# A depthwise convolution's three terms moved to ScalarE, its sums made in two long operations, and one Strassen-like step taken a unit later

## The chip, the cores and the metric

One Trainium2 chip, one core of it. The metric is the device time of the whole program in microseconds. In rows of the profile, PE is TensorE (matmuls), PEld its weight loads, DVE is VectorE, ACT is ScalarE, POOL is GpSimd and SP is SyncE, which here only issues DMAs. A "q" behind a name means the engine's sequencer. L896 is line 896 of the kernel file.

## The reference

A two-layer encoder on 256 tokens with 2048 features, all in float32. Each layer is an attention mixer and then a gated feed-forward block, each with a residual sum. The change touches the feed-forward block alone:

```python
D_FF = 5632
def conv_ffn(x, w_up, conv_w, conv_b, w_down):
    h = jnp.einsum("bsd,df->bsf", x, w_up)
    g, u = h[..., :D_FF], h[..., D_FF:]
    gp = jnp.pad(g, ((0, 0), (1, 1), (0, 0)))
    g = conv_w[0] * gp[:, :-2] + conv_w[1] * gp[:, 1:-1] + conv_w[2] * gp[:, 2:] + conv_b
    return jnp.einsum("bsf,fd->bsd", jax.nn.gelu(g) * u, w_down)
```

The gate `g` is convolved along the tokens with three taps for each feature, goes through the GELU and is multiplied with `u`.

## The kernel before

Every float32 matmul is made of three: operands are split into a high part (a rounded copy, made by a cast on ACT) and a low part (the rest, made by a subtraction on VectorE), and the products high x high, high x low and low x high are added in PSUM. Weights come from memory as units of 128 x 1024 (`raw`, five buffers, loaded on SP's queue); `split` makes `wh` on ACT (L231) and `wl` on VectorE (L234), four buffers each. A unit feeds 12 matmuls of 512 columns (`a_unit`, L195 to L197).

The up projection runs in 11 groups for each layer (`up_group`), each for 512 gate features (x = 0) and 512 `u` features (x = 1). A group takes eight steps over the contraction. The first four steps do both sides (`u` = 0 to 3), then come four for the gate side alone and four for the other side. At step `UPK` a group does not multiply plainly: `column_forms` combines the weights of the two sides with four sums on VectorE (L951, L952, L954, L955), splits the combinations as three pairs `wh`/`wl` and one quarter (`form`, from the tile `t`), and `seven_products` makes seven block products instead of eight (L977 to L979), 21 matmuls instead of 24. Four extra PSUM banks take products that are added to both sides later (`extra_parts`, `scaled_parts`).

When the gate side is done, VectorE evicts it (L878, into a tile of the tag `sc`), transposes it in blocks of 32 (L279), and 16 DMAs move the blocks (L273, twelve on POOL, four on SP) into `sides[0]`, a tile `qk` of four feature blocks by 256 tokens. The `u` side follows the same way through a tile `z` into `sides[1]`. Work that is to come later is put off with `later` and issued by `tick`: the convolution (`convolved`) is issued two ticks after the gate's eviction and so falls into the start of the next group, and `multiplied` comes there too. In three groups of each half (`HALVES`, groups 1 to 3 of the half) `multiplied` also makes the sums L324 to L327 and splits them for the down projection.

The convolution works on each of four feature blocks: ACT makes the middle term with the bias (L896), VectorE adds the two outer terms with a fused multiply-add each (L897, L899), over 255 tokens. Then one ACT operation makes the GELU of all four (L901).

The order of instructions on each engine is set by a scheduler at build time; it follows priorities and its own estimate of times. Each engine runs its list in order, so a waiting instruction holds up all behind it.

Of the kernel before, what the change touches and what calls it, by code (L numbers as in the profile page):

```python
# [29 lines left out]
AF = mybir.ActivationFunctionType  # L30
ALU = mybir.AluOpType
# [3 lines left out]
SEQ = 256  # L35
# [12 lines left out]
RAW = 5  # L48
AHEAD = 4
LAST = 2  # L50
UPK = 2
HALVES = ((0, 6, (1, 2, 3)), (6, 11, (1, 2, 3)))


# [17 lines left out]
def trunk_kernel(ctx: ExitStack, tc, a, out):  # L72
    nc = tc.nc
    V, S, G, T = nc.vector, nc.scalar, nc.gpsimd, nc.tensor
# [11 lines left out]
    def nm(s):  # L86
        uid[0] += 1
        return f"{s}_{uid[0]}"
# [22 lines left out]
    def load(name, shape, src=None, pool=const, tag=None, eng=G):  # L111
        t = pool.tile(list(shape), F32, name=name, **({"tag": tag} if tag else {}))
        tc.keep_in_program_order(eng.dma_start(t, a[name] if src is None else src))
        return t

    def tps(tag, bufs):
        return psum.tile([P, 512], F32, name=nm(tag), tag=tag, bufs=bufs)
# [164 lines left out]
    def y_tile(src, gain, kt, pin=False):  # L282
        y = acts.tile([P, 2, SEQ], F32R, name=nm("yT"), tag="yT", bufs=KT)
        dst = [y[:, x, :] for x in range(2)]
        if len(src.shape) == 3:
            dst = [d.rearrange("p (t q) -> p t q", t=2) for d in dst]
        split_scaled(*dst, src, gain[:, kt:kt + 1], pin)
        return y
# [16 lines left out]
    def turned_rows(c, gain, res):  # L305
# [6 lines left out]
        def tiles():  # L312
            for j in range(4):
                res[c * 4 + j] = y_tile(pf.rearrange("p (t j) q -> p j t q", t=2)[:, j], gain, c * 4 + j)
            if res is formed.get("of") and c == UPK // 2:
                y_forms(pf.rearrange("p (t j) q -> p j t q", t=2), gain)
# [4 lines left out]
    def form_sums(a11, a21, a12, a22):  # L321

        f = tmp.tile([P, 4, P], F32, name=nm("sums"), tag="scc")
        V.tensor_tensor(f[:, 0], a21, a22, op=ALU.add)  # L324
        V.tensor_tensor(f[:, 1], f[:, 0], a11, op=ALU.subtract)
        V.tensor_tensor(f[:, 2], a11, a21, op=ALU.subtract)
        V.tensor_tensor(f[:, 3], a12, f[:, 1], op=ALU.subtract)  # L327
        return f

    def y_forms(src, gain):  # L330

        y = tmp.tile([P, 2, 2, P], F32, name=nm("yf"), tag="ry")
        for k in range(2):
            S.activation(y[:, k], src[:, UPK % 2 * 2 + k], AF.Copy, scale=gain[:, 2 * UPK + k:2 * UPK + k + 1])
        f = form_sums(*(y[:, k, t] for k in range(2) for t in range(2)))
        form = []
        for x, tag in enumerate(("R", "Rq")):
            high = tmp.tile([P, 2, P], F32R, name=nm("form"), tag="t0")
            low = const.tile([P, 2, P], F32R, name=nm("form"), tag=tag, bufs=1)
            split(high, low, f[:, 2 * x:2 * x + 2])  # L340
            form += [(high[:, k], low[:, k]) for k in range(2)]
        formed["form"] = form

    def row_factor(pin=False, late=False):

        ss = tmp.tile([P, 2], F32, name=nm("ss"), tag="ss")
        ins = V.tensor_reduce(ss, ssq_now[0], axis=AX.X, op=ALU.add)
        if pin:
            tc.keep_in_program_order(ins)
        return rsqrt_mean(ss, D, "rstd", const, late=late)  # L350
# [63 lines left out]
    def quad(slot, dtype=F32):  # L414
        return att.tile([P, 4, SEQ], dtype, name=nm("qk"), tag=f"qk{slot}", bufs=1)
# [40 lines left out]
    def qk_tiles(srcs, act, rs, orders, slot):  # L456

        return [qk_sum(ps, r, order, slot + x)
                for x, (ps, r, order) in enumerate(zip(gemm_b(srcs, act), rs, orders))]
# [182 lines left out]
    def new_sc():  # L642
        return att.tile([P, 2, 512], F32, name=nm("sc"), tag="sc", bufs=1)
# [100 lines left out]
    convw = load("convw", (P, 2, 3, FT))  # L744
    convb = load("convb", (P, 2, FT))
# [89 lines left out]
    def up_group(layer, j, yT, rstd, prod, *more):  # L835
# [23 lines left out]
        for u in range(4):  # L859
            if not j and u == 2:  # L860
                rstd.append(row_factor())
            if u == UPK:
                extra += [tps("s", 2), tps("tp", 2), tps("tp", 2), tps("s", 2)]
# [6 lines left out]
        for x in range(2):  # L870
            for u in range(4, 8):
                a_unit(pss[x], src[x], u, yT, KT)
                if u % 2 == 1:
                    tick()
            z = (tmp.tile([P, 8, P], F32, name=nm("z"), tag="z", bufs=1) if x else
                 new_sc().rearrange("p t (f k) -> p (t f) k", k=P))
            for t in range(2):
                out = V.scalar_tensor_tensor(z.rearrange("p (f t) k -> p t f k", t=2)[:, t],  # L878
                                       pss[x][t].rearrange("p (f k) -> p f k", k=P), rstd[0][:, t:t + 1],
                                       sums[x][t].rearrange("p (f k) -> p f k", k=P), op0=ALU.mult, op1=ALU.add)  # L880
                if t:
                    tc.keep_in_program_order(out)
            sides[x] = quad(2 * x)
            turned(z.rearrange("p b k -> p (b k)"), sides[x].rearrange("p f (t k) -> p (f t) k", k=P), (3,))
            if not x:
                later(2, lambda: convolved(layer, j, sides))
        later(2, lambda: multiplied(j, sides, prod, *more))

    def convolved(layer, j, sides):

        g4, c4 = sides[0], quad(4)
        sides[2] = c4
        for i in range(4):
            f = 4 * j + i
            g, c = g4[:, i, :], c4[:, i, :]
            S.activation(c, g, AF.Identity, scale=convw[:, layer, 1, f:f + 1], bias=convb[:, layer, f:f + 1])  # L896
            V.scalar_tensor_tensor(c[:, 1:SEQ], g[:, 0:SEQ - 1], convw[:, layer, 0, f:f + 1],  # L897
                                   c[:, 1:SEQ], op0=ALU.mult, op1=ALU.add)
            V.scalar_tensor_tensor(c[:, 0:SEQ - 1], g[:, 1:SEQ], convw[:, layer, 2, f:f + 1],  # L899
                                   c[:, 0:SEQ - 1], op0=ALU.mult, op1=ALU.add)  # L900
        S.activation(c4, c4, AF.Gelu_apprx_tanh)  # L901

    def new_forms(g0, n):
# [254 lines left out]
    for hh in range(2):  # L1158
        vt = v_tiles(gemm_a(a["od_v"][hh], yT, KT), rstd, ((18, 19, 20, 21), (16, 17, 22, 23))[hh])
        for hd in range(hh * 4, hh * 4 + 4):  # L1160
# [9 lines left out]
            q, k = qk_tiles([a["od_qk"][hd * 2 + x] for x in range(2)], yT, (Rq, R), (rev, None), hd % 2 * 2)  # L1170
# [158 lines left out]
def _paired_up(w):  # L1329

    w = w.copy()
    x, y = w[:, :, 0, UPK].copy(), w[:, :, 1, UPK].copy()
    w[:, :, 0, UPK] = np.concatenate([x[..., :512], y[..., :512]], axis=-1)
    w[:, :, 1, UPK] = np.concatenate([y[..., 512:], x[..., 512:]], axis=-1)
    return w
# [71 lines left out]
```

## Time and profile before

| | |
|---|---|
| median of 3 runs | 2410.64 us (2410.23 to 2411.19) |
| the profiled execution | 2413.26 us, its span 2411.5 us |
| PE busy | 2394.5 us (99%) |
| VectorE busy | 1857.0 us (77%) |
| ACT busy | 1370.0 us (57%) |
| fused multiply-adds of the convolution (L897, L899) | 2 x 88, 479 and 478 ns each |
| ACT's term with the bias (L896) | 88, 591 ns each |
| GELU (L901) | 22, 1061 ns each |
| granted TensorE clock | 0.999 |

A row of the list of groups or of the timeline names the engine, the line, the operation, the tile that it writes and the tiles that it reads, and the shapes. In the timeline the first number is the start in us from the beginning of the span, the second how long the row lasts, `x4` says that four equal instructions are merged, and square brackets hold the idle time before it and what ended that. Engines overlap the end of an instruction with the start of the next, so the distance between two starts is shorter than a duration. In a view by stretches the columns are the stretch, its length, and the busy time (and instructions) of PE, PEld, DVE, ACT and POOL, then the clock, the DMA share and GB/s.

### The profile page before, as it was taken

To read this page: it belongs to the slowest core of one execution; us is meant where nothing else is said; L and a number is where in the kernel's file an instruction comes from. 1 tells how busy PE (TensorE), PEld (TensorE's weight loads), DVE (VectorE), ACT (ScalarE), POOL (GpSimd) and SP (SyncE) were. 2 spreads that over 40 slices of the span, in tenths; PEclk is the share of its full clock that TensorE was granted. 3 is DMA by queue.
4 is the path that set the end of the run, shared out by engine and by line. 5 is a ranking of instruction groups with operands and counts; after the bars stand their busy time and mean duration, and the time that the engine had idled before them with its cause. 6 is when DMAs were issued, how large, how long until landed. Compare 5 with 4: busy or idle time off the path is not lost.

```text
span 2411.5 us, 32978 instructions
## 1 busy us (share of the span) xinstructions
PE 2394.5 (99%) x10895; PEld 1981.0 (82%) x10895; DVE 1857.0 (77%) x2461; ACT 1370.0 (57%) x1954; POOL 540.0 (22%) x940
## 2 busy tenths in 40 slices
PE   9999999999999999999999999999999999999998
PEld 7888888888887888888788888888888888887787
DVE  6576566666778888778889867776788887788887
ACT  6455455566665565445656657555665654556564
POOL 1142032322222322004232100422223320033220
PEclk9999999999999999999999999999999999999999
DMA  8778678766767777668777764667677776677774
GB/s 306 205 196 239 199 194 240 219 197 186 213 198 220 219 210 213 203 207 217 206 226 209 223 200 139 193 193 212 196 218 227 211 220 201 203 223 207 230 211 156
DMA packets 287532, 505.65 MB, mean 210 GB/s; under 512 B 159096, under 2 KB 160504, under 8 KB 287360
## 3 DMA queue, kind: packets, MB, share of 16 engines
q1 hardware_dynamic: 256848, 470.15, 62.7%
q0 software_dynamic: 30080, 32.74, 8.0%
q8 instruction: 85, 1.39, 0.2%
q14 instruction: 87, 0.71, 0.1%
q10 hardware_dynamic: 432, 0.66, 0.1%
HBM read 458.48 MB, written 2.18 MB: 191 GB/s over the span
## 4 chain that ended last, share of the span: by engine, by line
PE 81%; DVE 6%; DMA 6%; issue 2%; ACT 2%; SPq 1%; POOL 1%; DVEq 0%; ACTq 0%; POOLq 0%
PE gm L196 22%; PE gm L197 22%; PE gm L195 22%; DMA qk<-sc 4%; DVE wl L234 2%; PE gm L145 2%; ACT wh L231 1%; SPq L273 1%; POOL qk L273 1%; PE tp L977 1%; PE gm L978 1%; PE gm L977 1%; PE gm L979 1%; PE tp L978 1%; PE tp L979 1%
## 5 line engine op out<-in xcount | busy, mean ns | idle before, releaser
L231 ACT CAST wh<-raw 128x1024 fp32r<-128x1024 f32 (+1 forms) x897 | 933.3, 1047 | 805.9 <-PE gm L197 619.5
L234 DVE TENSOR_TENSOR wl<-raw,wh 128x1024 fp32r<-128x1024 f32 (+1 forms) x897 | 1080.4, 1216 | 379.7 <-ACT wh L231 372.3
L196 PE MATMUL gm<-wl,yT 128*128 128x512 f32 x2092 | 816.1, 390 | 1.9 <-DVE wl L234 1.7
L195 PE MATMUL gm<-wh,yT 128*128 128x512 f32 x2092 | 816.3, 390 | 0.0
L197 PE MATMUL gm<-wh,yT 128*128 128x512 f32 x2092 | 814.8, 389 | 0.0
L196 PEld LDWEIGHTS gm<-wl,yT 128*128 128x128 f32 x2092 | 392.8, 188 | 87.8 <-DVE wl L234 7.7
L197 PEld LDWEIGHTS gm<-wh,yT 128*128 128x128 f32 x2092 | 392.7, 188 | 82.1 <-DVE yT L240 0.2
L195 PEld LDWEIGHTS gm<-wh,yT 128*128 128x128 f32 x2092 | 392.8, 188 | 81.3 <-ACT junk L265 0.4
L273 POOL DMA_DIRECT2D qk<-sc x264 | 152.2, 584 | 838.3 <-issue 365.2
L273 POOL DMA_DIRECT2D qk<-z x392 | 226.3, 585 | 287.5 <-DVE z L279 258.9
L195 PE MATMUL gm<-wh,prod 128*128 128x512 f32 x518 | 201.5, 389 | 0.0
L197 PE MATMUL gm<-wh,prod 128*128 128x512 f32 x518 | 201.5, 389 | 0.0
L196 PE MATMUL gm<-wl,prod 128*128 128x512 f32 x518 | 201.5, 389 | 0.0
L195 PEld LDWEIGHTS gm<-wh,prod 128*128 128x128 f32 x518 | 97.2, 188 | 20.4
L197 PEld LDWEIGHTS gm<-wh,prod 128*128 128x128 f32 x518 | 97.2, 188 | 20.2
L196 PEld LDWEIGHTS gm<-wl,prod 128*128 128x128 f32 x518 | 97.2, 188 | 20.2
L196 PE MATMUL gm<-wl,mix 128*128 128x512 f32 x256 | 100.1, 391 | 0.7 <-DVE wl L234 0.7
L195 PE MATMUL gm<-wh,mix 128*128 128x512 f32 x256 | 100.0, 391 | 0.0
L197 PE MATMUL gm<-wh,mix 128*128 128x512 f32 x256 | 99.6, 390 | 0.0
L273 POOL DMA_DIRECT2D hT<-z x72 | 41.5, 585 | 201.1 <-PE gm L197 76.8
L951 DVE TENSOR_TENSOR t<-raw 128x512 f32<-128x512 f32 x45 | 31.1, 690 | 39.4 <-DMA raw<-in_up 33.6
L145 PE MATMUL gm<-yT,wh 128*128 128x512 f32 x256 | 59.5, 390 | 0.0
(356 smaller groups left out, 2671.8 us busy)
## 6 DMA issues: line engine op xcount, KB each, us to landing
raw<-in_up SPq DMA_DIRECT2D x352, 512.0 KB, 4.5
raw<-in_down SPq DMA_DIRECT2D x176, 512.0 KB, 4.4
raw<-in_eva_qk SPq DMA_DIRECT2D x96, 512.0 KB, 4.4
raw<-in_eva_v SPq DMA_DIRECT2D x46, 512.0 KB, 5.7
raw<-in_evb_qk SPq DMA_DIRECT2D x32, 512.0 KB, 4.7
raw<-in_ev_out SPq DMA_DIRECT2D x32, 512.0 KB, 4.3
raw<-in_od_qk SPq DMA_DIRECT2D x32, 512.0 KB, 3.9
raw<-in_od_out SPq DMA_DIRECT2D x32, 512.0 KB, 4.5
```

The lines of the kernel that those rows point to most:

```text
L145: T.matmul(ps.rearrange("p a b -> p (a b)"), wh[:, k * P:(k + 1) * P], act[u * 8 + k].rearrange("p a b -> p (a b)"), start=(u == 0 and k = ...
L195: T.matmul(ps[t], ah, wh[:, sl], start=(kt == 0), stop=False)
L196: T.matmul(ps[t], ah, wl[:, sl], start=False, stop=False)
L197: T.matmul(ps[t], al, wh[:, sl], start=False, stop=(kt == nk - 1))
L231: first = S.copy(dst_h, src)
L234: V.tensor_tensor(dst_l, src, dst_h.bitcast(F32), op=ALU.subtract)
L273: (nc.sync if i in on_sync else G).dma_start(dst[j * 32:(j + 1) * 32, :, i * 32:(i + 1) * 32], z[i * 32:(i + 1) * 32].rearrange("p (b j c) ...
L951: V.tensor_tensor(t1, w12, w11, op=ALU.subtract)
L977: T.matmul(ps, ah, wh, start=own and first, stop=False)
L978: T.matmul(ps, ah, wl, start=False, stop=False)
L979: T.matmul(ps, al, wh, start=False, stop=own and last)
```

## The change

ACT makes all three terms: the middle one with the bias into `c4`, the first into a new tile of the tag `sc`, and the last in place over the gate. VectorE adds the two outer ones for all four feature blocks at once, 4 x 255 columns in each operation. And `UPK` becomes 3: the seven products are made at step 3 instead of step 2.

```diff
-UPK = 2
+UPK = 3
...
         g4, c4 = sides[0], quad(4)
         sides[2] = c4
-        for i in range(4):
-            f = 4 * j + i
-            g, c = g4[:, i, :], c4[:, i, :]
-            S.activation(c, g, AF.Identity, scale=convw[:, layer, 1, f:f + 1], bias=convb[:, layer, f:f + 1])
-            V.scalar_tensor_tensor(c[:, 1:SEQ], g[:, 0:SEQ - 1], convw[:, layer, 0, f:f + 1],
-                                   c[:, 1:SEQ], op0=ALU.mult, op1=ALU.add)
-            V.scalar_tensor_tensor(c[:, 0:SEQ - 1], g[:, 1:SEQ], convw[:, layer, 2, f:f + 1],
-                                   c[:, 0:SEQ - 1], op0=ALU.mult, op1=ALU.add)
+        before = new_sc().rearrange("p a (b q) -> p (a b) q", b=2)
+        for taps, dst in ((1, c4), (0, before), (2, g4)):
+            for i in range(4):
+                f = 4 * j + i
+                w = convw[:, layer, taps, f:f + 1]
+                if taps == 1:
+                    S.activation(dst[:, i, :], g4[:, i, :], AF.Identity, scale=w, bias=convb[:, layer, f:f + 1])
+                else:
+                    S.activation(dst[:, i, :], g4[:, i, :], AF.Copy, scale=w)
+        V.tensor_tensor(c4[:, :, 1:SEQ], c4[:, :, 1:SEQ], before[:, :, 0:SEQ - 1], op=ALU.add)
+        V.tensor_tensor(c4[:, :, 0:SEQ - 1], c4[:, :, 0:SEQ - 1], g4[:, :, 1:SEQ], op=ALU.add)
         S.activation(c4, c4, AF.Gelu_apprx_tanh)
```

Lines behind the convolution stand three lower in the changed file: L901 becomes L904 for the GELU, L928 becomes L931, L951 to L955 become L954 to L958, and L977 to L979 become L980 to L982. The two additions are L902 and L903.

The scheduler gives another order. The rows below are from the start of the third group of the first layer, where the convolution of the second group falls. ACT there, before (the first row is the first pair of the combined weights, the rows with `raw_6976` and `raw_6977` behind it the second and third):

```order
L231 CAST wh_6983<-raw_6977 128x1024
L896 ACTIVATE qk_6836<-qk_6746,convb,convw 128x256 x4
L231 CAST wh_6989<-raw_6976 128x1024
L901 ACTIVATE qk_6836<-qk_6836 128x1024
L231 CAST wh_6997<-raw_6977 128x1024
L231 CAST wh_7033<-raw_7031 128x1024
```

and now, where `wh_6980` and `wh_6998` are the plain weights of step 2, and `raw_7018` and `raw_7019` the combined ones of step 3:

```order
L231 CAST wh_6980<-raw_6978 128x1024
L899 ACTIVATE qk_6839<-qk_6749,convb,convw 128x256 x4
L901 ACTIVATE sc_6840<-qk_6749,convw 128x256 x4
L901 ACTIVATE qk_6749<-qk_6749,convw 128x256 x4
L231 CAST wh_6998<-raw_6996 128x1024
L231 CAST wh_7025<-raw_7019 128x1024
L904 ACTIVATE qk_6839<-qk_6839 128x1024
L231 CAST wh_7031<-raw_7018 128x1024
L231 CAST prod_6966<-qk_6839 128x256
```

Twelve operations in a row stand where four stood, and the casts of the second plain weights and of the combined weights have moved behind them. VectorE at the same place, before:

```order
L954 TENSOR_TENSOR raw_6977<-raw_6977,t_1277_6980 128x512
L234 TENSOR_TENSOR wl_6990<-raw_6976,wh_6989 128x1024
L955 TENSOR_TENSOR raw_6977<-raw_6977 128x512
L234 TENSOR_TENSOR wl_6998<-raw_6977,wh_6997 128x1024
L234 TENSOR_TENSOR wl_7034<-raw_7031,wh_7033 128x1024
L234 TENSOR_TENSOR wl_7052<-raw_7049,wh_7051 128x1024
L928 TENSOR_TENSOR qk_6836<-qk_6836,qk_6853 128x1024
L234 TENSOR_TENSOR wl_7074<-raw_7071,wh_7073 128x1024
```

and now, from the additions to the product:

```order
L902 TENSOR_TENSOR qk_6839<-qk_6839,sc_6840 128x4x255
L903 TENSOR_TENSOR qk_6839<-qk_6839,qk_6749 128x4x255
L234 TENSOR_TENSOR wl_6999<-raw_6996,wh_6998 128x1024
L234 TENSOR_TENSOR wl_7026<-raw_7019,wh_7025 128x1024
L957 TENSOR_TENSOR raw_7019<-raw_7019,t_1285_7022 128x512
L234 TENSOR_TENSOR wl_7032<-raw_7018,wh_7031 128x1024
L931 TENSOR_TENSOR qk_6839<-qk_6839,qk_6859 128x1024
L958 TENSOR_TENSOR raw_7019<-raw_7019 128x512
```

Behind them stand the four sums, the four `prod` splits and the three `form` splits, and only then the third pair (`wl_7040`) and the next plain unit (`wl_7076`):

```order
L234 TENSOR_TENSOR prod_6975<-qk_6839,prod_6975 128x256
L234 TENSOR_TENSOR form_7036<-t_1285_7022,form_7035 128x512
L234 TENSOR_TENSOR wl_7040<-raw_7019,wh_7039 128x1024
L234 TENSOR_TENSOR wl_7076<-raw_7073,wh_7075 128x1024
L845 TENSOR_TENSOR sum_7065<-sum_7064,tp_7016 128x512
```

The product with `u` (L928, now L931) stood behind the low halves of all combined weights and of the two units after them; now it stands ahead of the third pair. TensorE's order at the end of the seven products is now:

```order
L982 MATMUL s_7017<-wh_7031,form_5887 128x512
L980 MATMUL tp_7015<-form_7035,form_5882 128x512
L980 MATMUL tp_7016<-wh_7039,form_5882 128x512
L980 MATMUL gm_6878<-wh_7039,yT_5871 128x512
L981 MATMUL tp_7015<-form_7036,form_5882 128x512
L982 MATMUL tp_7015<-form_7035,form_5883 128x512
L195 MATMUL gm_6877<-wh_7075,yT_6025 128x512
L981 MATMUL tp_7016<-wl_7040,form_5882 128x512
L982 MATMUL tp_7016<-wh_7039,form_5883 128x512
L981 MATMUL gm_6878<-wl_7040,yT_5871 128x512
L982 MATMUL gm_6878<-wh_7039,yT_5871 128x512
```

The matmuls with the low weights of the third pair have moved behind the first one of the next plain unit; before, the matmuls of that pair that add to `gm` stood together, three in a row, ahead of the plain unit.

## The prediction

> **What bounds the kernel now.** I read the page first, then the start times of the matmuls, then the time from one gate eviction to the next (L878 into `sc`, one in each group), and last the waits inside one group.
>
> ```profile
> span 2411.5 us, 32978 instructions
> PE   2394.5 (99%) x10895; PEld 1981.0 (82%) x10895; DVE 1857.0 (77%) x2461; ACT 1370.0 (57%) x1954; POOL 540.0 (22%) x940
> ...
> 744.74 0.39 PE L195 MATMUL gm<-wh,yT 128*128 128x512 f32 x1
> ...
> 748.14 0.39 PE L195 MATMUL gm<-wh,yT 128*128 128x512 f32 x1
> ```
>
> TensorE is busy 99%, but that says little, since the matmuls overlap. Between the two starts quoted lie 15 matmuls in 3.40 us: 0.2267 us each is the undisturbed pace. A gain can only come from places where the pace breaks. In the up projections the gate evictions show how much that is (the first number of a row is the stretch from eviction to eviction, the second its length):
>
> ```profile
> 694.06:736.97 42.91, 42.91 (x190) 35.48 (x190) 35.95 (x47) 26.60 (x33) 13.82 (x24) 1.00 0.76 219
> 736.97:781.67 44.70, 43.78 (x190) 35.23 (x190) 37.51 (x52) 25.73 (x34) 13.84 (x24) 1.00 0.71 204
> 781.67:825.28 43.61, 43.55 (x191) 35.33 (x190) 37.27 (x51) 25.53 (x33) 13.83 (x24) 1.00 0.76 217
> ...
> 2197.74:2242.41 44.67, 43.77 (x191) 35.25 (x190) 37.28 (x51) 25.53 (x33) 13.83 (x24) 1.00 0.72 215
> 2242.41:2287.28 44.87, 43.92 (x191) 35.24 (x190) 37.54 (x52) 25.52 (x33) 16.03 (x28) 1.00 0.80 233
> sum 786.61, PE 782.21 PEld 635.92 DVE 664.09 ACT 461.74 POOL 251.14; mean PE 43.46 PEld 35.33 DVE 36.89 ACT 25.65 POOL 13.95
> ```
>
> A group is 189 matmuls, 42.85 us at that pace, and the undisturbed stretch is 42.91. The 18 stretches of this view sum to 786.61, so 786.61 - 18 x 42.91 = 14.2 us are stalls: all that the change can win here. They lie in the 12 stretches where the product of the group before also makes its sums (L324 to L327; "form groups" below); the others stand at 42.91 or close to it. One form group, around its stall:
>
> ```profile
> 761.76 0.40 PE L977 MATMUL gm<-wh,yT 128*128 128x512 f32 x1
> 762.90 0.50 PE L978 MATMUL gm<-wl,yT 128*128 128x512 f32 x1 [0.74 <-DVE wl L234]
> ...
> 764.04 0.50 PE L196 MATMUL gm<-wl,yT 128*128 128x512 f32 x1 [0.17 <-DVE wl L234]
> 764.38 0.39 PE L197 MATMUL gm<-wh,yT 128*128 128x512 f32 x1
> ```
>
> ```profile
> 754.13 2.08 ACT L896 ACTIVATE qk<-qk,convb,convw 128x256 f32<-128x256 f32 x4 [2.02 <-DMA qk<-sc]
> 756.12 1.04 ACT L231 CAST wh<-raw 128x1024 fp32r<-128x1024 f32 x1
> ```
>
> ```profile
> 754.77 0.98 DVE L897 SCALAR_TENSOR_TENSOR qk<-qk,convw,qk 128x255 f32<-128x255 f32 x2
> ...
> 758.03 0.69 DVE L954 TENSOR_TENSOR raw<-raw,t 128x512 f32<-128x512 f32 x1
> 758.63 1.22 DVE L234 TENSOR_TENSOR wl<-raw,wh 128x1024 fp32r<-128x1024 f32 x1
> 759.77 0.69 DVE L955 TENSOR_TENSOR raw<-raw 128x512 f32<-128x512 f32 x1
> 761.62 3.50 DVE L234 TENSOR_TENSOR wl<-raw,wh 128x1024 fp32r<-128x1024 f32 x3 [1.17 <-ACT wh L231]
> ```
>
> The chain is: the gate's transposed blocks land, ACT starts the convolution, VectorE works through eight fused operations, and only then come the steps that make the low halves of the combined weights, for which TensorE waits. Let T be the start of the group that the convolution falls in (748.14 here, always 11.17 us after the gate eviction) and c the time from T to ACT's first convolution operation (6.0 here). Then wl of the third pair ends at c + 8.7, and TensorE wants it at T + 13.8: a stall of about c - 5. The chain, not any engine's sum of work, makes these stalls.
>
> **The change part by part.** UPK = 3 moves the seven products one unit later: 24 matmuls x 0.2267 = 5.44 us more before the combined weights are wanted. It removes no matmul, no DMA and no bytes. On SP the two loads (L939, L940 before) come two loads later and stay ahead of the four moves of `z`; POOL's queue keeps its order. The other move is on VectorE, where the transpose of `z` no longer stands behind a weight subtraction.
>
> The convolution: VectorE loses eight operations and gains two of 1020 columns; ACT gains eight scaled copies of 256 columns.
>
> ```profile
> 650.17 1.71 ACT L237 ACTIVATE yT<-hT,ln 128x256 fp32r<-128x256 f32 x4 [1.09 <-DMA hT<-z]
> ...
> L334 ACT ACTIVATE yf<-hT,ln x4: 493/494/496, 636.4 to 1663.4; 128x256 f32<-128x256 f32 x4
> ...
> 765.04 1.22 DVE L928 TENSOR_TENSOR qk<-qk,qk 128x1024 f32<-128x1024 f32 x1
> 766.17 1.22 DVE L234 TENSOR_TENSOR wl<-raw,wh 128x1024 fp32r<-128x1024 f32 x1
> 767.31 0.28 DVE L324 TENSOR_TENSOR sums<-qk 128x128 f32<-128x128 f32 x1
> 767.51 0.28 DVE L326 TENSOR_TENSOR sums<-qk 128x128 f32<-128x128 f32 x1
> ...
> 768.45 0.42 DVE L234 TENSOR_TENSOR prod<-qk,prod 128x256 fp32r<-128x256 f32 x1
> 768.79 0.42 DVE L234 TENSOR_TENSOR form<-sums,form 128x256 fp32r<-128x256 f32 x1
> ```
>
> From start to start: four Identity operations 1.99 (0.50 each); a scaled copy (1.71 - 0.49)/3 = 0.40; a VectorE operation of 1024 columns 1.14, of 512 0.60 (758.03 to 758.63), of 256 0.34, of 128 0.20; a fused one of 255 (758.03 - 754.77 = 3.26 for eight) 0.41. For the 1020 columns I take 1.14, four columns being nothing. The scaled copies write in place and read the moves' target, which no row shows; their ends are 0.31 (a cast of 256, below) and 0.50 (the Identity with its bias).
>
> By the sum of work the trade is even: VectorE saves 8 x 0.41 - 2 x 1.14 = 1.0 us in a group, ACT pays 8 x 0.40 = 3.2, and both have room (DVE 37 of 44 us, ACT 26). The path is what counts. ACT does the three terms one after the other, and the last addition needs the last term: tap 1 takes 1.99, the eight copies end at c + 5.28, the second addition starts at c + 5.33. Before, VectorE was through with the convolution at c + 3.9; now at c + 6.5. So 2.6 of the 5.44 us are spent at once.
>
> The Trainium skill, ScalarE: Activation LUTs, Rules for kernel authors, says to put additions and multiplications on VectorE, not ScalarE, with VectorE up to about three times as fast for single-source bf16. In this fp32 case the rows do not agree on the rate (0.40 against 0.41), so the sum goes by the rows; as an estimate from that page, at a third of 0.41 the eight operations would be worth only 1.1 us to VectorE against 3.2 paid on ACT, and the change would lose 2.1 us more in each of the 22 groups in which ACT is late.
>
> From the second addition on VectorE is without a gap in a form group, in the order that now stands: addition 1.14, subtraction of the second plain weights and of the first pair 2 x 1.14, L957 0.60, subtraction of the second pair 1.14, the product with `u` 1.14, L958 0.60, four sums 0.80, four `prod` splits 1.34, the `form` splits 1.20, the third pair's subtraction 1.14, the next unit's 1.22. That is 12.6, and the last ends at c + 5.33 + 12.6 = c + 17.9. The product and its splits, which before stood behind the combined weights, now stand ahead of the third pair. The product starts at c + 10.5, here 16.5 after T against 16.9 today (765.04), and the moves of `z` that it needs start 1.14 earlier, so I add no wait for their landing.
>
> ```profile
> 763.39 0.58 ACT L844 COPY sum<-s 128x512 f32<-128x512 f32 x1
> 763.87 1.05 ACT L231 CAST wh<-raw 128x1024 fp32r<-128x1024 f32 x1
> ...
> 766.29 1.33 ACT L231 CAST prod<-qk 128x256 fp32r<-128x256 f32 x4 [1.37 <-DVE qk L928]
> 767.52 0.61 ACT L231 CAST form<-t 128x512 fp32r<-128x512 f32 x1
> 768.04 0.40 ACT L231 CAST form<-sums 128x256 fp32r<-128x256 f32 x1
> ```
>
> ACT waits for the same product, which ends at c + 11.7: four casts 1.23, the `form` casts 2 x 0.52, the third pair's cast about 0.95, the copy 0.48, the next unit's cast 1.05: c + 16.5.
>
> TensorE at its pace reaches the seven products at T + 16.3, the quarter from `form` at T + 19.04, the next unit's high weights at T + 20.17 and its low ones at T + 21.53. With 0.1 us from an operation's end to TensorE (761.62 + 1.22 to 762.90), the high ones come at c + 16.6 and the low ones at c + 18.0. Both give a stall of c - 3.5. After a wait the next matmul is 0.1 late again (764.04 to 764.38, 0.34 instead of 0.23).
>
> What is c? In the 12 form groups, taken as at 754.13:
>
> ```profile
> 2213.03 1.09 ACT L896 ACTIVATE qk<-qk,convb,convw 128x256 f32<-128x256 f32 x2
> ...
> 2259.75 2.08 ACT L896 ACTIVATE qk<-qk,convb,convw 128x256 f32<-128x256 f32 x4 [2.20 <-DMA raw<-in_up]
> ...
> ACT qk L896 <- DMA qk<-sc: 10.9, 15, 2.0
> ```
>
> it runs from 4.1 (2213.03 less 2208.91) to 6.2 (2259.75 less 2253.58), mean 4.9. It is set by the landing (15 of 22 times the wait is for it) and the change leaves those moves alone, so I keep it. The 12 form groups then stall 12 x (4.9 - 3.5 + 0.1) = 18.0 us. In the other 10 there are no sums and no `form` splits of them ahead of the third pair; by the same sum they stall c - 4.45, with c from 3.9 to 5.1: together 1.4 us, where they have almost none now. The stalls of today, 14.2, go, because the combined weights themselves are now in time up to the third pair.
>
> Sum: 18.0 + 1.4 - 14.2 = +5.2 us. The profiled execution took 2413.26 (its span 2411.5), 2.62 above the median of 2410.64. So 2418.5 there, and 2415.8 as a median.
>
> Both ends: with copies of 0.31 the second addition starts 0.7 earlier, with 0.50 it starts 0.8 later: -9 to +10 us over the 12 groups.
>
> **The rivals.** (a) The stalls only shrink or stay as large: c or the chain is 0.1 to 0.8 us shorter than summed, and the time is within 0.2% (4.8 us, about what a measurement of this kernel can tell from no change). For it: the sum is a difference of two nearly equal terms. About 2411.
> (b) Faster: the later deadline covers everything, all 14.2 us go and none come: 2410.6 - 14.2 = 2396. For it: 5.44 us of new room. It decides where the low weights of the next unit are ready by T + 21.5, for the mean c 1.4 us before my sum; against it: twelve operations in a row on ACT, and the product ahead of the third pair. Half of it, 2403, would need 0.7 us.
> (c) Slower by much: ACT's block holds up the plain weight casts behind it, or the gate lands late. The second plain cast ends at c + 6.2 and is wanted at T + 13.6, so ACT itself is late only from c = 7.3, above the largest of today. But if the moves, now beside loads that start earlier, land at 6.0 to 6.2 everywhere, as in two of 12 today, the form groups stall 2.7 each and the others 1.6: 32 + 16 - 14 = +34, 2445. The page's rule would lead here too.
>
> **How the numbers follow.** My forecast, slower by a little, 2415.8: 0.40; (a) 0.38; (b) and its half 0.17; (c) 0.05. Slower is the forecast and (c). The range takes the ends of the copies, 2407 to 2426, a little lower for half of (b): 2405 to 2426.
>
> **What would show it.** The stretches between gate evictions: about 44.4 in form groups and near 43.0 in the others if I am right, all 42.91 under (b). In a form group TensorE's waits should have moved from the third pair after the eviction to the matmuls of the third pair and of the first plain unit behind it, released by ACT wh or DVE wl, and VectorE should be without a gap from the second addition to there. ACT's copies should stand 0.40 apart, and the additions should last 1.22. I am wrong if the gate lands at another time than today, or if the scheduler's order leaves VectorE time that I did not see.

## The result, and the profile after

The changed kernel took 2424.16 us (median of 4 runs, 2423.43 to 2426.0), the kernel before 2410.91 (4 runs, 2410.23 to 2413.92): a ratio of 1.0051, 95% interval 1.0038 to 1.0063. It is slower by 13 us. The sign and the mechanism were forecast and the time lies in the range, but the loss is more than twice the 5.2 us forecast. The profiled execution took 2424.23 us, its span 2422.5, so it stands at its median, while the profiled one of before stood 2.6 us above its own: 11.0 us from profile to profile. One execution behind the times below, of UPK = 3 with the product two ticks later, took 2636 us at a granted clock of 0.85; it enters no ratio.

The page of the changed kernel, and its groups for the convolution (the last columns are busy time, mean ns of one, idle time of the engine just before and what ended it):

```profile
span 2422.5 us, 33004 instructions
PE 2400.2 (99%) x10895; PEld 1978.5 (82%) x10895; DVE 1846.1 (76%) x2329; ACT 1435.2 (59%) x2130; POOL 539.2 (22%) x940
...
L901 ACT ACTIVATE qk<-qk,convw 128x256 f32<-128x256 f32 x88 | 37.3, 495 | 0.0
L901 ACT ACTIVATE sc<-qk,convw 128x256 f32<-128x256 f32 x88 | 37.3, 494 | 0.0
L903 DVE TENSOR_TENSOR qk<-qk,qk 128x1020 f32<-128x1020 f32 x22 | 26.9, 1221 | 8.2 <-ACT qk L901 5.3 <-DMA qk<-z 2.9
L902 DVE TENSOR_TENSOR qk<-qk,sc 128x1020 f32<-128x1020 f32 x22 | 26.9, 1221 | 32.8 <-ACT sc L901 32.8
```

VectorE works 11 us less and ACT 65 us more. But VectorE stands idle 41 us in front of the two additions, 38 of which the trace puts down to waits for ACT's terms. Before, its first fused operation had 1.9 us of such idle time:

```profile
L897 DVE SCALAR_TENSOR_TENSOR qk<-qk,convw,qk 128x255 f32<-128x255 f32 x88 | 38.8, 479 | 1.9 <-ACT qk L896 1.7
```

The stretches between gate evictions, as in the prediction, for the changed kernel:

```profile
692.64:735.56 42.92, 42.92 (x190) 35.48 (x189) 35.48 (x41) 29.60 (x41) 13.77 (x24) 1.00 0.75 217
735.56:780.48 44.92, 43.89 (x190) 35.17 (x189) 36.89 (x46) 28.73 (x42) 13.80 (x24) 1.00 0.77 206
...
1726.72:1770.65 43.93, 43.47 (x190) 35.24 (x189) 35.33 (x40) 29.60 (x41) 13.80 (x24) 1.00 0.75 209
...
2118.16:2162.42 44.26, 43.46 (x190) 35.32 (x189) 35.42 (x40) 28.21 (x40) 13.80 (x24) 1.00 0.77 208
2251.26:2297.12 45.86, 44.45 (x190) 35.10 (x189) 36.83 (x45) 28.63 (x41) 15.98 (x28) 1.00 0.79 229
sum 793.66, PE 785.41 PEld 634.50 DVE 655.02 ACT 515.92 POOL 250.42; mean PE 43.63 PEld 35.25 DVE 36.39 ACT 28.66 POOL 13.91
```

793.66 - 18 x 42.91 = 21.3 us of stalls, where 14.2 were: 18.5 of them in the 12 form groups (mean stretch 44.45), 2.8 in the six others. The rest of the program is five long stretches: the one ahead of the first gate eviction and the four that begin with the last group of a half, whose convolution falls in the down projection (first the sum of before, then the four and the sum of after):

```profile
sum 1624.89, PE 1612.28 PEld 1345.10 DVE 1192.91 ACT 908.29 POOL 288.83; mean PE 322.45 PEld 269.02 DVE 238.58 ACT 181.66 POOL 57.77
```

```profile
911.64:1083.30 171.66, 170.42 (x748) 139.97 (x747) 133.11 (x144) 89.01 (x102) 13.81 (x24) 1.00 0.67 204
1258.00:1726.72 468.72, 466.43 (x2298) 393.62 (x2297) 359.08 (x540) 281.15 (x483) 87.84 (x147) 1.00 0.66 196
1947.72:2118.16 170.44, 170.07 (x748) 140.05 (x747) 133.02 (x144) 88.88 (x102) 13.79 (x24) 1.00 0.69 205
2297.12:2422.50 125.38, 117.58 (x521) 96.50 (x519) 103.00 (x130) 68.80 (x99) 13.84 (x24) 0.99 0.61 186
sum 1628.84, PE 1614.74 PEld 1344.00 DVE 1191.06 ACT 919.28 POOL 288.82; mean PE 322.95 PEld 268.80 DVE 238.21 ACT 183.86 POOL 57.76
```

These four are 1.9, 1.5, 0.9 and 1.2 us longer than before, 5.4 together; the start is 1.4 shorter (694.06 to 692.64). So 7.1 + 5.4 - 1.4 = 11.0 us: the whole difference.

One form group of after (T = 735.56 + 11.17 = 746.73, c = 752.01 - 746.73 = 5.3), ACT, VectorE and TensorE in the timeline:

```profile
752.01 2.08 ACT L899 ACTIVATE qk<-qk,convb,convw 128x256 f32<-128x256 f32 x4 [1.35 <-DMA qk<-sc]
754.00 1.70 ACT L901 ACTIVATE sc<-qk,convw 128x256 f32<-128x256 f32 x4
755.60 1.70 ACT L901 ACTIVATE qk<-qk,convw 128x256 f32<-128x256 f32 x4
```

```profile
755.73 1.22 DVE L902 TENSOR_TENSOR qk<-qk,sc 128x1020 f32<-128x1020 f32 x1 [1.46 <-ACT sc L901]
757.33 1.22 DVE L903 TENSOR_TENSOR qk<-qk,qk 128x1020 f32<-128x1020 f32 x1 [0.38 <-ACT qk L901]
...
762.60 1.22 DVE L931 TENSOR_TENSOR qk<-qk,qk 128x1024 f32<-128x1024 f32 x1
...
767.16 0.69 DVE L234 TENSOR_TENSOR form<-t,form 128x512 fp32r<-128x512 f32 x1
767.76 2.36 DVE L234 TENSOR_TENSOR wl<-raw,wh 128x1024 fp32r<-128x1024 f32 x2
```

```profile
766.07 0.49 PE L980 MATMUL tp<-form,form 128*128 128x512 f32 x1 [0.15 <-ACT form L231]
767.32 0.50 PE L980 MATMUL tp<-wh,form 128*128 128x512 f32 x1 [0.76 <-ACT wh L231]
...
768.75 0.50 PE L195 MATMUL gm<-wh,yT 128*128 128x512 f32 x1
```

The copies stand 1.60/4 = 0.40 apart. From the second addition to the low weights of the next plain unit VectorE has no gap, and TensorE waits at the third pair.

### The profile page after: what moved, and what is told of

Read it like the earlier page. It is cut to its first block, busy times and chain, and to the rows that moved or that the text cites. A ratio compares the mean times of both kernels' runs of the same rounds, so it can differ in the third digit from the quotient of the medians.

```text
span 2422.5 us, 33004 instructions
## 1 busy us (share of the span) xinstructions
PE 2400.2 (99%) x10895; PEld 1978.5 (82%) x10895; DVE 1846.1 (76%) x2329; ACT 1435.2 (59%) x2130; POOL 539.2 (22%) x940
## 5 line engine op out<-in xcount | busy, mean ns | idle before, releaser
L856 ACT ACTIVATE sum<-sum,rstd 128x512 f32<-128x512 f32 x88 | 58.9, 716 | 10.8 <-DVE sum L847 9.9
L231 ACT CAST prod<-qk 128x256 fp32r<-128x256 f32 x88 | 29.2, 403 | 52.5 <-DVE qk L931 52.5
```

What stands on the lines that cost most here:

```text
L231: first = S.copy(dst_h, src)
L856: S.activation(sums[x][t], sums[x][t], AF.Copy, scale=rstd[0][:, t:t + 1])
```

## The experiments

Below, "stalls" are all the time by which matmul starts in a group's 31.5 us from T on fall behind the undisturbed pace, summed from the starts in the trace (before: 13.2 us in form groups and 0.5 behind the ten others; changed kernel: 18.4 and 7.4). Times are medians; each ratio is to the kernel before, measured beside it, whose median was 2410.1 to 2411.9.

**UPK = 3 alone.**

```diff
-UPK = 2
+UPK = 3
```

> UPK = 3 alone, with the convolution of before (ACT one term, VectorE eight fused operations). Theory: the loss comes from the convolution's long series on ACT, which ends 2.6 us later and leaves the third pair and the next plain unit late, and not from the later step. Here VectorE is through with the convolution at c + 3.9, the third pair's low half is ready about T + 16.3 and the next unit's about T + 19.6, wanted at T + 20.6 and T + 21.5: nearly all of the 13.6 us of stalls of before go and none come, about 2397 to 2400 us. Rival: the later step costs in itself (the additions of the extra banks, the loads or the product get in each other's way at their new places), whatever the convolution is: 2410 or more.

2410.93 us, ratio 0.9997 (0.9989 to 1.0006). The rival held: the later step by itself gains nothing. Form groups stall 12.3 us, the others 0.2. The chain of the prediction is gone from them, though: the wait is at another place, the quarter `form`, whose low half the scheduler put behind the product and its splits. In the group shown the product also waits for `u` (in four of the 12 for more than 0.2 us):

```profile
851.83 1.22 DVE L928 TENSOR_TENSOR qk<-qk,qk 128x1024 f32<-128x1024 f32 x1 [1.14 <-DMA qk<-z]
...
859.13 0.68 DVE L234 TENSOR_TENSOR form<-t,form 128x512 fp32r<-128x512 f32 x1
```

```profile
859.87 0.50 PE L978 MATMUL tp<-form,form 128*128 128x512 f32 x1 [1.15 <-DVE form L234]
```

**The convolution alone.**

```diff
-UPK = 3
+UPK = 2
```

(against the changed kernel)

> The new convolution alone, UPK = 2 as before. In the order that stands here the four combining sums and the low half of the first pair are ahead of the two additions, so the third pair's low half ends at c + 8.8 (before c + 8.7) and the stall in the form groups is about c - 4.9 as before. Theory: the convolution's lateness costs only where something needed stands behind it: form groups about as before (13 us), the four groups whose convolution falls in the start of the down projection lose the 4.6 us that they lose in the changed kernel: about 2413 to 2418 us. Rival: the 2.6 us by which the convolution ends later come on top of every stall: 12 x 2.6 = 31 us more, about 2442.

2414.90 us, ratio 1.0012 (1.0003 to 1.0021). The theory held: form groups stall 10.4 us, the ten others 7.4, of which 5.7 in the four groups that run into the down projection. So the parts do not add up: step alone -0.2, convolution alone +3.8, both +13. In the changed kernel's order the product stands ahead of the third pair's low half, in this run's behind it: form groups stall 18.4 and 10.4 us.

**The product two ticks later,** with the new convolution and with the old one:

```diff
-        later(2, lambda: multiplied(j, sides, prod, *more))
+        later(4, lambda: multiplied(j, sides, prod, *more))
```

> The changed kernel with the product with u issued two ticks later, so that its sums and the splits of them stand behind the next plain unit's low half. Theory: what delays the third pair and the next unit is the product with its eleven small operations (4.5 us of VectorE time) ahead of them: the next unit's low half moves from c + 17.9 to about c + 16.5, the third pair's to c + 14, and the stall in form groups from c - 3.5 to about c - 5: 18.4 us become 2 to 3, the down projection keeps its 4.6: about 2403 to 2407 us. Rival: the twelve operations in a row on ACT are late by themselves (the casts behind them), the place of the product does not matter: 2418 or more.

> The convolution of before, UPK = 3, and the product two ticks later. Theory: without the late convolution neither place of the product causes a stall, so this is within 2 us of UPK = 3 alone, about 2397 to 2400. Rival: the product has to wait and then holds up the additions of the extra banks and the next eviction: 2405 or more.

> The convolution of before, UPK = 3, the product two ticks later, for its profile. Theory: no stall over 0.1 us in any up projection group (form groups 12 to 18 us in the other versions, here under 1.5), nor in the four groups whose convolution falls in the down projection; about 2399 to 2401 us. Rival: part of the gain comes from somewhere else than these stalls (attention, output), then the stretches between gate evictions still stand above 43.2 in form groups.

With the new convolution 2423.05 us, ratio 1.0042 (1.0029 to 1.0056): the rival's time. With the old one 2399.74, ratio 0.9951 (0.9937 to 0.9965), and measured a second time, for its profile, 2400.20, ratio 0.9955 (0.9941 to 0.9968), with 1.6 us of stalls in form groups, all in one group whose c was 8.1, and 0.2 in the others. The time is the one expected; the reason given for it was not right, since the product's place does matter: 11 us lie between this and UPK = 3 alone. So they are there to be had, as rival (b) said, and the order that came with the product's place withheld them in the run with UPK = 3 alone.

With the new convolution the same move mostly shifts the waits further back (of TensorE there: us in total, times, longest):

```profile
PE gm L195 <- ACT wh L231: 6.5, 4, 1.8
PE gm L196 <- DVE wl L234: 4.2, 8, 1.0
```

The second row is the low weights of the plain units behind the seven products, for which VectorE is still late. The first row is not at the next plain unit, as the expectation of the run after this one has it, but behind it, 26 us after T, in the first form group of each half: ACT's cast stands behind an operation on the sums of the extra banks (L856), and that waits for an addition of VectorE's:

```profile
1160.91 0.72 ACT L856 ACTIVATE sum<-sum,rstd 128x512 f32<-128x512 f32 x1 [0.47 <-DVE sum L847]
1161.54 1.03 ACT L231 CAST wh<-raw 128x1024 fp32r<-128x1024 f32 x1
```

VectorE's low half for a unit there ends at the same time (26.1 us after T in this group), so both engines are late. The profiled execution took 2418.38 us, the fastest of six, with 16.2 us of stalls in form groups and 4.0 in the others; what the others lost beyond that, no trace shows.

**The product three ticks later,** `later(5, ...)`, new convolution.

> The changed kernel with the product three ticks later, so that on both engines the next plain unit's halves stand ahead of the splits of the product (with two ticks, ACT's four casts of the product still stood ahead of that unit's cast, and TensorE waited there up to 2.0 us). Theory: the convolution's late end costs only through the product and its splits ahead of the weights; VectorE then has the next unit's low half at about c + 15.2 and ACT its high half at about c + 13, wanted at T + 21.5 and T + 20.2, with c about 4.7: no stalls in the up projections; the four groups in the down projection keep their 4 to 5 us: about 2402 to 2406 us. Rival: the twelve operations in a row on ACT make everything behind them late, wherever the product is: 2415 or more.

2409.63 us, ratio 0.9994 (0.9985 to 1.0003): between the two, and level with the kernel before. Most of the stalls go, but 6.1 us stay in form groups (nearly all in the four with c from 5.1 to 6.3) and 3.1 in the down projection. VectorE's queue is late as far as the third unit behind the seven products (TensorE waits for its low weights 28 us after T). My estimate was some 5 us too low: it followed the queue no further than the first.

**Eight of the gate's moves on SP.**

```diff
-            turned(z.rearrange("p b k -> p (b k)"), sides[x].rearrange("p f (t k) -> p (f t) k", k=P), (3,))
+            turned(z.rearrange("p b k -> p (b k)"), sides[x].rearrange("p f (t k) -> p (f t) k", k=P), (3,) if x else (1, 3))
```

> The changed kernel, with eight of the gate's 16 moves on SP and eight on POOL (now four and twelve). Theory: c, the landing of the gate's blocks, sets every stall. POOL's last move is issued 2.3 us earlier, c falls from 4.7 to about 2.0 to 2.5, and a stall of c - 3.3 in form groups and c - 3.6 to c - 4.3 elsewhere vanishes: about 2397 to 2405 us. The order on ACT changes too (the convolution now stands ahead of two plain casts). Rival: landing is set by the DMA engines, which are 75% busy, and not by the issue; c stays near 4.7, the convolution waits ahead of the plain casts, the loads behind the moves on SP come later: 2424 or more.

2424.02 us, ratio 1.0053 (1.0039 to 1.0066). Neither held. The gate landed about 6 us earlier and c fell from 4.8 to about -1.2 in most groups, and still the form groups stalled 17.9 us and the ten others 7.8. The scheduler had moved the load of the second raw unit (L943) behind the moves of `z` on SP; it was issued at 1790.87 here, 5.0 after T, and VectorE waited for it ahead of the combined weights:

```profile
1788.21 2.55 SPq L273 DMA_DIRECT2D qk<-z  x4
1790.87 0.54 SPq L943 DMA_DIRECT2D raw<-in_up  x1
```

```profile
1796.15 0.69 DVE L955 TENSOR_TENSOR raw<-raw,raw 128x512 f32<-128x512 f32 x1 [0.95 <-DMA raw<-in_up]
```

In form groups the product starts 15.6 us after T on average, in the changed kernel 15.3, now held by this load or by the landing of `u`:

```profile
DVE qk L931 <- DMA qk<-z: 8.6, 9, 2.2
```

So c sets the stall only while it is the last to come; that it can be bought off without a new wait is not shown.

**The last tap fused on VectorE,** with the product in the change's place, and two ticks later:

```diff
-        for taps, dst in ((1, c4), (0, before), (2, g4)):
+        for taps, dst in ((1, c4), (0, before)):
...
-        V.tensor_tensor(c4[:, :, 0:SEQ - 1], c4[:, :, 0:SEQ - 1], g4[:, :, 1:SEQ], op=ALU.add)
+        for i in range(4):
+            f = 4 * j + i
+            V.scalar_tensor_tensor(c4[:, i, 0:SEQ - 1], g4[:, i, 1:SEQ], convw[:, layer, 2, f:f + 1],
+                                   c4[:, i, 0:SEQ - 1], op0=ALU.mult, op1=ALU.add)
```

> The changed kernel with the same edit (ACT two terms, VectorE four fused operations for the last tap), the product where the change has it. On VectorE the order from the first addition to the next plain unit is as in the changed kernel, the idle time before the second addition is gone but the fused operations are 0.5 us longer: the product starts at about c + 10.3 (changed kernel: c + 10.6). Theory: VectorE's queue decides, so the stalls in form groups fall by 0.2 to 0.3 us each only: 2419 to 2424 us. Rival: the twelve operations in a row on ACT are the cause; with four fewer everything behind them is 1.6 us earlier and most stalls go: 2408 or less.

> As the changed kernel with the product two ticks later, but ACT makes only two terms (eight operations, its series ends at c + 3.65 and not c + 5.28) and VectorE adds the last tap with four fused operations of 255 columns (1.64 us in place of 1.14). VectorE is through with the convolution at about c + 7.6 (a plain low half stands between), ACT with its block 1.6 us earlier than in that kernel. Theory now: what is late is VectorE's queue behind the convolution, because VectorE stands idle 1.9 us in a group until ACT's terms are there; here that idle time is nearly gone (the plain low half stands between), and the next unit's cast stands ahead of the product's casts: about 2400 to 2407 us. Rival: the convolution's end on VectorE alone counts, which is no earlier here: 2418 or more.

In the change's place: 2420.30 us, ratio 1.0042 (1.0029 to 1.0056), product at c + 10.44. The theory held: ACT's last four operations are not what costs most. Form groups still stall 16.5 us, with the same order on VectorE behind the convolution. Two ticks later: 2413.86 us, ratio 1.0014 (1.0005 to 1.0023), between theory and rival, with 9.9 and 5.0 us of stalls. I had expected VectorE's idle time to be nearly gone; it was not, since the addition came first and waited for ACT's second term:

```profile
DVE qk L902 <- ACT sc L901: 37.3, 22, 3.7
```

**The same with the fused operations first.**

```diff
-        V.tensor_tensor(c4[:, :, 1:SEQ], c4[:, :, 1:SEQ], before[:, :, 0:SEQ - 1], op=ALU.add)
         for i in range(4):
             f = 4 * j + i
             V.scalar_tensor_tensor(c4[:, i, 0:SEQ - 1], g4[:, i, 1:SEQ], convw[:, layer, 2, f:f + 1],
                                    c4[:, i, 0:SEQ - 1], op0=ALU.mult, op1=ALU.add)
+        V.tensor_tensor(c4[:, :, 1:SEQ], c4[:, :, 1:SEQ], before[:, :, 0:SEQ - 1], op=ALU.add)
```

> The kernel with two terms on ACT, four fused operations on VectorE and the late product once more (2413.9 us), with the two outer taps in the other order on VectorE: the four fused operations first, which need only ACT's first four terms and the gate, and the addition of 1020 columns behind them. The same operations on both engines, no one more or less. VectorE is through with the convolution at about c + 4.9 and not at c + 6.4 (c + 7.6 with the plain low half between). Theory: the idle time of VectorE ahead of its first operation of the convolution, 37 us in 22 groups there, is what makes its queue late; it nearly goes, and the stalls of 14.8 us in the up projections and behind them fall to about 2: about 2400 to 2404 us. Rival: ACT's eight operations in a row or the sum of work make the stalls, the order of the taps does not matter: 2411 or more.

2399.19 us, ratio 0.9953 (0.9939 to 0.9967). The theory held: the same operations in another order of the taps, and 15 us are gone. This is as fast as the old convolution with the late product (2399.74 and 2400.20), so no run shows that moving terms to ACT gains anything by itself. VectorE's idle time in front of the convolution is 2.1 + 6.6 us, and the 18 stretches are the undisturbed 18 x 42.91 = 772.4:

```profile
L904 DVE SCALAR_TENSOR_TENSOR qk<-qk,convw,qk 128x255 f32<-128x255 f32 x88 | 37.3, 479 | 2.1 <-DMA qk<-z 1.5 <-ACT qk L899 0.6
L906 DVE TENSOR_TENSOR qk<-qk,sc 128x1020 f32<-128x1020 f32 x22 | 26.9, 1222 | 6.6 <-ACT sc L901 6.5
...
sum 772.35, PE 772.35 PEld 638.69 DVE 661.12 ACT 490.10 POOL 251.14; mean PE 42.91 PEld 35.48 DVE 36.73 ACT 27.23 POOL 13.95
```

The scheduler's order also moved with it: in most groups a weight's low half that stood between the two parts of the convolution now stands behind them, and the quarter's low half one sum earlier. So the run shows these together.

**The new convolution in the last group of each half only,** UPK = 3 and the product in the change's place (under the condition stands the new convolution, under the other branch that of before):

```diff
+        if j in (5, 10):
...
+        else:
...
```

> UPK = 3 and the product where the change has it, with the new convolution only in the last group of each half (four in the program), whose convolution falls in the start of the down projection, and the convolution of before in the other 18. UPK = 3 alone took 2410.9 us with 0.2 us of stalls behind the groups that are not form groups. Theory: the part of the loss that my sum left out is made by the new convolution in these four groups alone: 0.8 to 1.4 us of stalls behind each, 4 to 5 us together, no new ones in the up projections: about 2414 to 2417 us. Rival: these stalls were landing times of that execution, they do not come with the convolution: 2409 to 2412 us.

2415.61 us, ratio 1.0016 (1.0007 to 1.0025), 4.7 above UPK = 3 alone, or 3.8 when each is taken against the kernel before measured beside it. Behind the four groups stand 1.4, 0.6, 0.9 and 1.1 us of stalls, behind the other six that are not form groups none. The theory held.

## Why the prediction was right, and where it was mis-sized

**The mechanism held, step by step.** In the group shown the second addition starts at c + 5.32 (worked out: 5.33), the product at c + 10.59 (10.5), the next unit's low half ends at 767.76 + 2.36 - 752.01 = c + 18.1 (17.9). In the 12 form groups c has a mean of 4.8 (4.9 taken), and the stall follows it one for one: 0.7 us at c = 3.9, 2.0 at 5.3, 2.9 at 6.1, about c - 3.2 where the sum had c - 3.4. The term of 18.0 us came out at 18.5, at the matmuls named. The price of a scaled copy, taken at 0.40, was 0.40. The Trainium skill (ScalarE: Activation LUTs, Rules for kernel authors) states VectorE's advantage, up to about three times, for bf16 and operations with a single source. The trace shows none here, in fp32 and with a fused operation of two sources: 494 ns for a copy of 256 columns on ACT, 479 ns for a fused operation of 255 on VectorE. So the estimate that the prediction made from that figure did not apply.

**The term for the other ten groups was mis-sized:** 1.4 us in the sum, 7.4 in the stalls. Four of these groups have their convolution in the start of the down projection, and I priced them with the up projection's deadlines and order. That was the wrong step. In the first of them the product starts at c + 11.9, after 1.3 us of idle time on VectorE. The trace names no cause, but the last block of `u` had landed only 0.5 us before; the prediction put a wait for that at nothing, and no other of the 22 groups shows one. The quarter's low half stands behind the product and its splits, and VectorE, from there without a gap, is late again for the next seven products 12 us further on:

```profile
939.09 1.22 DVE L931 TENSOR_TENSOR qk<-qk,qk 128x1024 f32<-128x1024 f32 x1 [1.26 <-issue]
```

```profile
942.91 0.50 PE L981 MATMUL tp<-form,form 128*128 128x512 f32 x1 [0.70 <-DVE form L234]
...
955.14 0.50 PE L981 MATMUL tp<-qk,form 128*128 128x512 f32 x1 [0.37 <-DVE qk L234]
```

They cost 4.6 us in stalls, for which the sum had 1.2 (its c - 4.45 where c was 4.84, 4.58 and 5.09); the run with the new convolution in these groups alone shows 4.0 of it. The other six cost 2.8 in the stretches, for which the sum had 0.2, mostly because the gate landed later in two of them (c of 5.2 and 5.6 where the trace of before had 4.4 and 4.1): the spread of c, which I left at one execution's values.

**The step from profile to median** took off 2.6 us by which the profile of before stood above its median; that of after stood at its own. So 5.8 us of the miss of 8.4 are the sum's (mainly the two points above), and 2.6 are this. That the time still lay in the range, 1.8 us from its upper end, owes something to luck: the range was made from the price of a scaled copy, which was right, and these misses had no place in it.

**The rivals.** (a), no change, and (c), +34 us, did not come. (b) came, not for this change but for two variants of it: all stalls of today go once the product is out of the way and VectorE starts the convolution early. What I did not name is what ties these together: not ACT's twelve operations as such, but that VectorE, whose queue is full for 12 us behind the convolution, starts on it 3.7 us after c, where before it started 1.2 us after c on average, and stands idle meanwhile. The prediction counted that lateness rightly and put it down to the length of ACT's series. The runs with UPK = 3, as the difference in us of the median to that of the kernel before measured beside it:

| VectorE starts at | product in the change's place | two ticks later | three ticks later |
|---|---|---|---|
| c + 1.1 | old convolution -0.2 | old convolution -11.3 and -9.9; fused operations first -12.7 | not run |
| c + 3.7 | the change +13.3; last tap fused +9.4 | +12.0; last tap fused +3.0 | -0.4 |

With the product at the same place the early start is always faster. It is not the only way: three ticks later the late start too comes back to the time of before.

**Still open:** how much of the 25 us between the changed kernel and the run with the fused operations first is VectorE's start and how much the scheduler's new order; each edit moved both. The fused operations first with the product in the change's place were not run.

## What to carry to other kernels

When a chain of work goes over two engines, ask when the busier one can take its first step, not only how much work it loses: here it lost 11 us of work and gained 39 us of idle time in front of the convolution, and the order of two taps, with what the scheduler made of it, was worth 15 us. A deadline that is moved later is worth nothing if the scheduler fills the new room with something else; look at what now stands ahead of the operation that is wanted. And price each group where its work really falls: the four at the seam between two phases had other deadlines than the rest.

## What the hardware showed unexpectedly

With eight of the gate's 16 moves on POOL's queue and not twelve, POOL's last was issued 2.3 us earlier, yet the gate landed about 6 us earlier. The median time from issue to landing on that queue fell from 5.3 us to 2.2 (a row: number of moves, KB of each, median us to landing; first the changed kernel, then the run with eight):

```profile
qk<-sc POOLq DMA_DIRECT2D x264, 32.0 KB, 5.3
```

```profile
qk<-sc POOLq DMA_DIRECT2D x176, 32.0 KB, 2.2
```

The Trainium skill (DMA: Bandwidth & Descriptors, Anatomy of one DMA) gives about 2.0 us and the bytes at 436 KB/us for one DMA of GpSimd's path, as an estimate 2.1 us for 32 KB: the row with eight agrees, the row with twelve does not.

That the number of moves makes the difference is not shown. In the changed kernel the first four of POOL's twelve landed in 2.0 to 2.5 us as well (medians of the 22 groups by place in the row); from the fifth on it was 4.6 to 6.4. The fifth is issued 5.6 us after the gate eviction, and SP, through with its four moves, issues the next two loads of 512 KB 5.4 and 6.0 us after it. With eight moves on SP these loads come 8.0 and 8.7 us after the eviction, behind POOL's last move. One group of each, the changed kernel first (eviction at 780.48, then at 1774.66):

```profile
783.74 6.90 POOL L273 DMA_DIRECT2D qk<-sc  x12 [26.80 <-issue]
785.85 1.02 SPq L128 DMA_DIRECT2D raw<-in_up  x2
```

```profile
1777.37 5.17 SPq L273 DMA_DIRECT2D qk<-sc  x8
1782.64 1.01 SPq L128 DMA_DIRECT2D raw<-in_up  x2
```

So the loads may be what the later moves wait for. No run moved the loads alone.
